# Feed-forward groups of 4, 5, 5, 5 and 3 chunks in a two-layer hybrid encoder: one more chunk multiplied by quads, another home for the down products' inputs

## Chip, cores and metric

The kernel runs on one core of a Trainium2 chip. The metric is device microseconds of one execution; "time" below is the median of three executions.

## What is computed

Two layers of an encoder trunk on 512 tokens of width 1024, all in float32. Cut to what matters:

```python
for l in range(2):
    h = rms_norm(x, attn_norm_g[l])
    proj = h @ w_in[l]                      # latents, GQA q/k/v, pool channels, gates
    merged = sum(gate_b * (branch_b @ w_branch_b[l]) for b in (mla, gqa, pool))
    x = x + merged @ w_out[l]
    hf = rms_norm(x, ffn_norm_g[l])
    u = depthwise_conv3(hf @ ffn_w_up[l]) + bias      # width 2 * 2816
    x = x + (silu(u[:, :2816]) * u[:, 2816:]) @ ffn_w_down[l]
```

The change touches the last three lines, the feed-forward part, in both layers.

## The kernel before

**Products.** Features stand on the 128 partitions, tokens along the free dimension (512). Each float32 operand is split into a high part of type float32r and a low part (the rest), and each product is three matmuls: high by high, high by low, low by high (`mm3`). So one product of 128x128 weights with 512 tokens is three matmuls of 512 columns. `HH` and `HL` hold the normed input's two parts, `wh`/`wl` and `fh`/`fl` the weights' parts. All matmuls are recorded at L526.

**Order.** The program is written out by hand, engine by engine, while a model of the engines' clocks (`Clock`) runs beside it: a side chain (`chain`, started `after` some microseconds) puts its instructions on DVE, ACT and POOL when that model's time has come. It sets only the order; on the chip the engines wait for each other by semaphores.

**Feed-forward, in 22 chunks of 128 columns of the gate half and 128 of the value half.** The chunks are cut into groups by `SIZES`, five of them. Those of the first group are "plain": two units of 8 products of 512 tokens each, 48 matmuls of 512 columns a chunk. All later chunks are "formed": the width of 1024 is paired off into four quads (two feature blocks by two halves of the tokens), and each quad takes seven products of 256 tokens in place of eight, by sums and differences of weights and of inputs. That is 7 x 4 x 3 = 84 matmuls of 256 columns a chunk. The sums of the inputs (`tf`, `hn`, `tt`) are made once a layer by `build_forms`, a quad at a time, as soon as the quad's two feature blocks are there; those of the weights by `w_form`, chunk by chunk. For three of the seven forms the low part is made by POOL issuing a transfer that adds the raw weights to minus the high part (`fl<-raw`, L438; the same for `wl<-raw` of other weights).

**Down products.** Each chunk's activations (`act`, or `ah` and `al`: high and low) meet 8 blocks of `ffn_w_down`. A group's down products, 8 per chunk, are dealt out among the next group's forms, behind the forms 22, 2, 4 and 3; those of the last group and 2 of the 8 output blocks of the group before it (`KEEP`) stand at the end of the layer. `keep_act` gives each chunk's activations a place: `PLACE[g] + i` below `ROOM` is one of 12 pieces of the four tiles of pool `mp` (which hold q and k in the attention), two per chunk; others go to `ah` from pool `wp` (tiles of 528 floats) and `al` from the slots `sp` (512 floats).

**Weights.** `_stream` sets the order in which the raw weights come over SP's queue. A formed chunk's four blocks are slots of their own; during the plain chunks the first of these are pulled ahead, one per plain unit. The split of weights runs 6 units ahead of TensorE in the feed-forward part (`LAF`).

**The norm.** The output projection's eight blocks m (`ps_acc`, `ps_ST`, `ps_AV` in turn) end in `resid` (`XM`), then `HH`, `HL` and the squares (`sqt`, summed into `sq` on POOL). `norm_begin` transposes the sum (`sqT`) and reduces it to `prt`; `norm_finish` puts a small matmul of `prt` between those of a plain unit when the model's time is `D_SUM` past `prt` (`D_FIRST` for the first norm of all), and from it come the per-token factors (`fac`, `rbc`), which scale the plain and formed results after the matmuls. So TensorE goes on with unscaled inputs while the norm is worked out. The norms are numbered `gen` 0 to 3: 0 and 2 ahead of the attention, 1 and 3 ahead of the feed-forward part.

Of the kernel before, what the change touches and what calls it, by code (L numbers as in the profile page):

```python
# [11 lines left out]
F32R = mybir.dt.float32r  # L12
# [6 lines left out]
P = 128  # L19
T = 512  # L20
# [10 lines left out]
WIDE = 528  # L31
# [10 lines left out]
PRE_A = 16  # L42
PRE_B = 8
LA, LAP, LAF = 3, 4, 6
SIZES = (5, 5, 5, 4, 3)
PLACE = (0, 5, 0, 5, 0)
ROOM = 6
KEEP = 2
FORMS = ("11", "12", "1", "22", "2", "4", "3")
# [8 lines left out]
D_SUM, D_FIRST = 2.0, 2.4  # L58
# [52 lines left out]
def _groups():  # L111
    e = np.cumsum(SIZES)
    return [(int(b - n), int(b)) for n, b in zip(SIZES, e)]


def _ffn():
# [4 lines left out]
    for g, (c0, c1) in enumerate(_groups()):  # L121
        dealt = len(late) - (KEEP * SIZES[g - 1] if g == len(SIZES) - 1 else 0)
        for n, c in enumerate(range(c0, c1)):
# [14 lines left out]
def _layer_units():  # L138

    r = _widths()  # L140
    for tok in _ffn():
        if tok[0] == "u":
            r += [("u", T), ("p", T), ("next",)]
        elif tok[0] == "f":
            r.append(tok)
        elif (tok[2] * SIZES[tok[1]] + tok[3]) % 4 == 0:
            r.append(("u" if tok[1] < len(SIZES) - 1 else "p", T))
    return r


def _stream():
# [4 lines left out]
    for kind, *u in _layer_units() * L:  # L156
        if kind == "next":
            plain = (plain + 1) % (2 * SIZES[0])
            if plain and plain >= 2 * SIZES[0] - 8:
# [49 lines left out]
class Clock:  # L209
# [37 lines left out]
    def done(self, *key):  # L247
        self.ready[key] = self.fin + self.SEM

    def need(self, *keys):  # L250
        for k in keys:
            while k not in self.ready:
                self.pop()
            self.to(self.ready[k])
# [4 lines left out]
    def chain(self, *steps, after=0.2):  # L259

        def go(n, source=None):
            if n == len(steps):
                return
            keys, fn = steps[n] if isinstance(steps[n], tuple) else ((), steps[n])
            late = [self.ready.get(k, self.now + 0.5) for k in keys]
            if late and max(late) > self.now:
                self.at(max(late) - self.now, lambda: go(n))
                return
            self.fin, self.source, self.last = self.now, source, None
            fn()  # L270
            source, self.source = self.last, None
            self.at(max(0.0, self.fin - self.now), lambda: go(n + 1, source))
        self.at(after, lambda: go(0))
# [65 lines left out]
def trunk(ctx: ExitStack, tc: tile.TileContext, x, w, prm, gb, cst, out):  # L339
    nc = tc.nc  # L340
    ctx.enter_context(tc.manual_schedule())
    ck = Clock()
    at, need, done, chain = ck.at, ck.need, ck.done, ck.chain
# [3 lines left out]
    cp = ctx.enter_context(tc.tile_pool(name="cp", bufs=1))  # L347
    rawp = ctx.enter_context(tc.tile_pool(name="rawp", bufs=RAW))
    hlp = ctx.enter_context(tc.tile_pool(name="hlp", bufs=LA + 3))
    sp = ctx.enter_context(tc.tile_pool(name="sp", bufs=NSLOT))  # L350
    wp = ctx.enter_context(tc.tile_pool(name="wp", bufs=NWIDE))
    sm = ctx.enter_context(tc.tile_pool(name="sm", bufs=2))
# [3 lines left out]
    uid = [0]  # L356

    def slot(name, dt=F32):
        uid[0] += 1
        t = sp.tile([P, SLOT], dt, tag="s", name=f"{name}_{uid[0]}")  # L360
        return t
# [5 lines left out]
    def small(name, shape, dt=F32, bufs=2):  # L367
        uid[0] += 1
        t = sm.tile(shape, dt, tag=name, name=f"{name}_{uid[0]}", bufs=bufs)
        return t  # L370
# [4 lines left out]
    def ps(tag):  # L375
        while not banks[tag]:
            ck.pop()
        ck.to(heapq.heappop(banks[tag]))
        uid[0] += 1
        t = pp.tile([P, T], F32, tag=tag, name=f"ps_{tag}_{uid[0]}", bufs=nbank[tag])  # L380
        return t
# [8 lines left out]
    def free(tag):  # L390
        heapq.heappush(banks[tag], ck.fin + ck.SEM)

    def f(ap):
        return ap.bitcast(F32)
# [130 lines left out]
    def mm(o, lhsT, rhs, start, stop, again=False):  # L525
        PE.matmul(o, lhsT=lhsT, rhs=rhs, start=start, stop=stop, skip_group_check=again)  # L526
        n = rhs.shape[-1]
        ck.to(ck.now + (n / 2400.0 + 0.0133 if st["ffn"] else max(0.107, n / 2370.0)))
# [20 lines left out]
    keep = cp.tile([P, 1], F32, tag="keep", name="keep")  # L549


    mp = ctx.enter_context(tc.tile_pool(name="mp", bufs=4))

    prms = []
    for l in range(L):
        t = cp.tile([P, NPRM], F32, tag=f"prm{l}", name=f"prm{l}")
# [60 lines left out]

    def norm_finish(gen, out, force=False):

        if gen not in parts or not (force or ck.ready.get(("prt", gen), 1e9) + (D_SUM if gen else D_FIRST) <= ck.now):  # L620
            return
        need(("prt", gen))
        s2 = ps("S")
        mm(s2[:, :16], C[:, C_GRP:C_GRP + P], parts.pop(gen), True, True)
        a, a4 = small("fac", [P, 16]), small("fac4", [P, 16])
        rt, rbc = out["rt"], out["rbc"] = small("rt", [P, 4]), slot("rbc")

        def mean():
            V.tensor_scalar(a, s2[:, :16], 1.0 / D, EPS, ALU.mult, ALU.add)
            free("S")  # L630

        def tokens():
            V.tensor_tensor(a4, a, C[:, C_SEL:C_SEL + 16], ALU.mult)
            V.tensor_reduce(rt, a4.rearrange("p (b g) -> p b g", g=4), AX.X, ALU.add)
            done("rt", gen)

        def rows():
            V.transpose(rbc[:, :T].rearrange("p (j r) -> p j r", r=32), bc(a.unsqueeze(2), [P, 16, 32]))
            done("rbc", gen)

        chain(mean, lambda: G.tensor_tensor(a, a, bc(mhalf, [P, 16]), ALU.pow), tokens, rows, after=0.3)
# [13 lines left out]
    parts = {}  # L655

    def bc(ap, shape):
        return ap.to_broadcast(shape)
# [26 lines left out]
    def layer(l, sq, xsrc):  # L685
# [3 lines left out]
        def col(i):  # L689
            return pr[:, i:i + 1]  # L690
# [146 lines left out]
        for g in range(4):  # L837
            acc = ps(ptags[g])
            for n, _ in enumerate(feat_major(acc, G1)):
                norm_finish(G1, nrm, g == 1 and n == 7)  # L840
            chain(*pool_steps(g, acc, ptags[g]))
# [748 lines left out]
        def build_forms(q):  # L1590
            a, b = slot("hn")[:, :T], slot("hn")[:, :T]
            lo, hi = slice(0, 256), slice(256, 512)
            t = (slot("tt")[:, :T], slot("tt")[:, :T])

            def whole():
                for k, z in ((2 * q, a), (2 * q + 1, b)):
                    V.tensor_scalar(z, XM[:, k, :], col(PRM_FG + k), None, ALU.mult)

            def sums():
                V.tensor_tensor(t[0][:, lo], a[:, hi], a[:, lo], ALU.subtract)  # L1600
                V.tensor_tensor(t[1][:, lo], b[:, hi], a[:, hi], ALU.subtract)
                V.tensor_tensor(t[0][:, hi], b[:, hi], t[0][:, lo], ALU.subtract)
                V.tensor_tensor(t[1][:, hi], b[:, lo], t[0][:, hi], ALU.subtract)

            def halves_of(name):
                i, h = {"1": (0, lo), "2": (0, hi), "3": (1, lo), "22": (1, hi)}[name]
                d = slot("tf", F32R)[:, :T]
                forms[name, q] = d[:, lo], d[:, hi]

                def low():  # L1610
                    V.tensor_tensor(d[:, hi], t[i][:, h], f(d[:, lo]), ALU.subtract)
                    done("tf", l, name, q)
                return [lambda: A.activation(d[:, lo], t[i][:, h], AF.Copy), low]

            for name, k, h in (("11", 2 * q, lo), ("12", 2 * q + 1, lo), ("4", 2 * q + 1, hi)):
                forms[name, q] = HH[:, k, h], HL[:, k, h]
                done("tf", l, name, q)
            chain(whole, sums, *[z for name in ("1", "2", "22", "3") for z in halves_of(name)], after=2.0)

        for m in range(KC):  # L1620
            tag = tags[m % 3]
            acc = ps(tag)
            for kc in range(KC):
                if kc % 4 == 0:
                    wh, wl = wnext()
                need(("mrg", l, kc))
                ws = slice((kc % 4) * P, (kc % 4) * P + P)
                mm3(acc, wh[:, ws], wl[:, ws], merged[kc][0][:, :T], merged[kc][1][:, :T], kc == 0, kc == KC - 1)

            def resid(m=m, acc=acc, tag=tag):  # L1630
                V.scalar_tensor_tensor(XM[:, m, :], acc, 0.5, XM[:, m, :], ALU.mult, ALU.add)
                free(tag)

            chain(resid, *norm_steps(G2, m, col(PRM_FG + m), sq),
                  *[lambda m=m: build_forms(m // 2)] * (m % 2))
# [14 lines left out]
        def keep_act(c):  # L1650
            g = next(i for i, (c0, c1) in enumerate(groups) if c0 <= c < c1)
            i = c - groups[g][0]
            n = 2 * (PLACE[g] + i)
            if n < 2 * ROOM:
                return places[n], places[n + 1]
            uid[0] += 1
            return wp.tile([P, WIDE], F32R, tag="w", name=f"ah_{uid[0]}")[:, :T], slot("al", F32R)[:, :T]

        def convolve(c, part, u):
            ci = c + part * FC  # L1660
# [353 lines left out]
```

## Time and profile before

| | |
|---|---|
| time, median of 3 executions | 1552.65 us (1552.56 to 1552.98) |
| the profiled execution | 1550.6 us |
| its span, first to last instruction | 1548.8 us, 1.8 us shorter |
| granted TensorE clock, mean | 1.000 |
| matmuls in the trace | 8265 |
| feed-forward part of layer 0 | from about 426.4 to 776.3 us of the span |
| of layer 1 | from about 1196.5 us to the end |

In the profile's rows, PE is a matmul on TensorE, PEld a weight load that runs beside it, DVE, ACT and POOL are the other engines, and SP issues transfers. A timeline row has the start in us, the time taken, engine, line, operation, output and inputs, the shape and the number merged into the row; in brackets stands the idle time ahead of it and what ended that. The ends of matmuls are modelled, so what a matmul costs in a stream is read from start to start. A windows row has, for a stretch, each engine's busy time and number of instructions, the granted clock, the share of the DMA engines that was busy, and GB/s.

### The profile page before, as it was taken

The numbers are of one execution on the slowest core, as the hardware profiler recorded it, in microseconds if no ns is written. First come the engines' busy times: TensorE is split into PE (matmuls) and PEld (weight loads), VectorE is DVE, ScalarE is ACT, GpSimd is POOL, SyncE is SP. The second block draws the span as 40 slices with busy tenths as digits, with TensorE's granted clock in tenths as the row PEclk, the third lists the DMA queues.
The fourth block names the chain that finished last, engine by engine and source line by source line (L and its number), as shares of the span: only waits on it lengthen the run. The fifth ranks groups of instructions, "written<-read, shape, count | busy, mean of one in ns | idle before, by whom it ended". The sixth has DMA issues, their size and how long they took to land.

```text
span 1548.8 us, 24353 instructions
## 1 busy us (share of the span) xinstructions
PE 1542.1 (100%) x8265; PEld 1341.3 (87%) x8265; DVE 1156.3 (75%) x1936; ACT 1066.5 (69%) x1994; POOL 775.3 (50%) x828
## 2 busy tenths in 40 slices
PE   9999999999999999999999999999999999999999
PEld 8888888888878999999898888888888899999997
DVE  6877886776687887877756678868667778888785
ACT  5557875877657877777644577758776677777772
POOL 3984886753453323222488648776535432222223
PEclk9999999999999999999999999999999999999999
DMA  5432344658968878886434323447598688787853
GB/s 203 123 120 82 88 123 141 162 128 207 225 164 195 197 169 181 197 192 143 128 128 131 111 75 92 125 144 175 117 216 213 169 205 186 180 187 177 212 116 102
DMA packets 138509, 241.26 MB, mean 156 GB/s; under 512 B 30864, under 2 KB 53392, under 8 KB 138384
## 3 DMA queue, kind: packets, MB, share of 16 engines
q1 hardware_dynamic: 91152, 162.93, 34.0%
q0 software_dynamic: 42336, 76.56, 28.8%
q8 instruction: 65, 1.06, 0.3%
q10 hardware_dynamic: 4896, 0.21, 0.2%
q14 instruction: 60, 0.49, 0.1%
HBM read 149.41 MB, written 13.63 MB: 105 GB/s over the span
## 4 chain that ended last, share of the span: by engine, by line
PE 92%; DVE 3%; DMA 2%; ACT 1%; issue 1%; POOL 1%; SPq 0%; ACTq 0%; POOLq 0%; DVEq 0%
PE ps_acc L526 40%; PE ps_AV L526 17%; PE ps_ST L526 15%; PE ps_S L526 10%; PE ps_mi L526 9%; DMA raw<-w 1%; DVE tf L307 1%; ACT wh L300 0%; SPq L862 0%; POOL wl L307 0%; DVE ctl L311 0%; DVE win L307 0%; ACT mx L300 0%; DVE wl L307 0%; POOL fac L307 0%
## 5 line engine op out<-in xcount | busy, mean ns | idle before, releaser
L438 POOL DMA_DIRECT2D wl<-raw x192 | 172.4, 903 | 383.1 <-ACT sx L300 163.7
L307 POOL TENSOR_TENSOR wl<-raw,wh 128x512 fp32r<-128x512 f32 (+2 forms) x171 | 219.9, 1294 | 179.4 <-ACT wh L300 171.7
L300 ACT ACTIVATE wh<-raw 128x512 fp32r<-128x512 f32 (+2 forms) x453 | 266.3, 605 | 55.6 <-DMA raw<-w 13.2
L438 POOL DMA_DIRECT2D fl<-raw x102 | 89.0, 873 | 155.2 <-ACT fl L300 62.6
L526 PE MATMUL ps_acc<-HH,wh 128*128 128x512 f32 x416 | 163.2, 392 | 0.5 <-DVE XM L311 0.4
L526 PE MATMUL ps_acc<-HL,wh 128*128 128x512 f32 x416 | 162.8, 391 | 0.3 <-DVE HL L311 0.3
L526 PE MATMUL ps_acc<-HH,wl 128*128 128x512 f32 x416 | 162.7, 391 | 0.0
L311 DVE SCALAR_TENSOR_TENSOR a<-u,prm,a 128x511 f32<-128x511 f32 x176 | 133.5, 761 | 33.5 <-ACT a L300 32.5
L300 ACT ACTIVATE wl<-wh 128x512 fp32r<-128x512 f32 x192 | 120.6, 628 | 6.1
L315 DVE TENSOR_REDUCE nm<-ps_S 128x1 fp32r<-128x512 f32 x128 | 87.8, 686 | 44.6 <-PE ps_S L526 43.7
L300 ACT ACTIVATE a<-u,prm 128x512 f32<-128x512 f32 x88 | 71.2, 811 | 57.2 <-DVE u L307 57.1
L526 PE MATMUL ps_acc<-tf,wh 128*128 128x256 f32 x544 | 100.1, 282 | 0.0
L526 PEld LDWEIGHTS ps_acc<-tf,wh 128*128 128x128 f32 x544 | 88.5, 189 | 6.2
L526 PEld LDWEIGHTS ps_acc<-HH,wh 128*128 128x128 f32 x416 | 78.4, 188 | 16.6 <-issue 0.7
L526 PEld LDWEIGHTS ps_acc<-HH,wl 128*128 128x128 f32 x416 | 78.2, 188 | 16.8
L526 PEld LDWEIGHTS ps_acc<-HL,wh 128*128 128x128 f32 x416 | 78.3, 188 | 16.6 <-DVE HL L311 0.6
L307 DVE TENSOR_TENSOR wl<-raw,wh 128x512 fp32r<-128x512 f32 (+2 forms) x91 | 66.2, 729 | 22.9 <-ACT wh L300 22.7
L526 PE MATMUL ps_AV<-HH,wh 128*128 128x256 f32 (+1 forms) x248 | 82.2, 331 | 0.0
L526 PE MATMUL ps_AV<-HH,wl 128*128 128x256 f32 (+1 forms) x248 | 82.1, 331 | 0.0
L526 PE MATMUL ps_AV<-HL,wh 128*128 128x256 f32 (+1 forms) x248 | 82.1, 331 | 0.0
L526 PE MATMUL ps_acc<-tf,wl 128*128 128x256 f32 x272 | 76.7, 282 | 0.0
L307 DVE TENSOR_TENSOR pl<-ps_ST,ph 128x512 fp32r<-128x512 f32 x86 | 58.3, 682 | 15.6 <-ACT ph L300 11.4
(426 smaller groups left out, 4975.3 us busy)
## 6 DMA issues: line engine op xcount, KB each, us to landing
raw<-w SPq DMA_DIRECT2D x160, 512.0 KB, 3.9
wl<-raw POOLq DMA_DIRECT2D x188, 256.0 KB, 4.4
raw<-w SPq DMA_DIRECT2D x140, 256.0 KB, 4.4
fl<-raw POOLq DMA_DIRECT2D x102, 256.0 KB, 5.6
raw<-w SPq DMA_DIRECT2D x14, 384.0 KB, 3.0
XM<-x SPq DMA_DIRECT2D x16, 256.0 KB, 4.5
dtq<-tr SPq DMA_DIRECT2D x16, 192.0 KB, 2.0
dtk<-tr SPq DMA_DIRECT2D x16, 192.0 KB, 3.3
```

Source lines behind the costliest of these rows:

```text
L300: return self.eng.activation(out, in_, func, **k)
L307: return self.eng.tensor_tensor(out, *a)
L311: return self.eng.scalar_tensor_tensor(out, *a)
L315: return self.eng.tensor_reduce(out, in_, *a, **k)
L438: nc.gpsimd.dma_start(f(lo), r, accum_op=ALU.add)
L526: PE.matmul(o, lhsT=lhsT, rhs=rhs, start=start, stop=stop, skip_group_check=again)
```

## The change

`SIZES` goes from 5, 5, 5, 4, 3 to 4, 5, 5, 5, 3: in each layer one chunk of the first group is no longer plain but formed, and the fourth group has five chunks. `PLACE` follows: the second group's first chunk now has place 4, so that two of its five chunks fit below `ROOM`. The pool `mp` is opened ahead of the slots and no longer behind them, and activations without a place take two slots, none of the wide tiles. The distance of the feed-forward norms' small matmul goes from 2.0 to 2.4 us of the model's time, and the sums of the third and fourth quad's inputs are started 8 us behind their block's chain in place of 2.

```diff
-SIZES = (5, 5, 5, 4, 3)
-PLACE = (0, 5, 0, 5, 0)
+SIZES = (4, 5, 5, 5, 3)
+PLACE = (0, 4, 0, 5, 0)
...
     hlp = ctx.enter_context(tc.tile_pool(name="hlp", bufs=LA + 3))
+    mp = ctx.enter_context(tc.tile_pool(name="mp", bufs=4))
     sp = ctx.enter_context(tc.tile_pool(name="sp", bufs=NSLOT))
     wp = ctx.enter_context(tc.tile_pool(name="wp", bufs=NWIDE))
...
-    mp = ctx.enter_context(tc.tile_pool(name="mp", bufs=4))
-
...
-        if gen not in parts or not (force or ck.ready.get(("prt", gen), 1e9) + (D_SUM if gen else D_FIRST) <= ck.now):
+        if gen not in parts or not (force or ck.ready.get(("prt", gen), 1e9) + (D_FIRST if gen in (0, 1, 3) else D_SUM) <= ck.now):
...
-            chain(whole, sums, *[...], after=2.0)
+            chain(whole, sums, *[...], after=2.0 if q < 2 else 8.0)
...
-            uid[0] += 1
-            return wp.tile([P, WIDE], F32R, tag="w", name=f"ah_{uid[0]}")[:, :T], slot("al", F32R)[:, :T]
+            return slot("ah", F32R)[:, :T], slot("al", F32R)[:, :T]
```

Nothing outside the two feed-forward parts and the norms ahead of them changes its order on any engine but for a few transfers of SP at the parts' ends. In the built programs 8261 matmuls become 8333: in each layer 48 of 512 columns go and 84 of 256 come. Per layer the down products between the forms go from 144 to 142, at the end from 32 to 34. The four `mp` tiles move from byte 204640 of each partition to byte 93824. The first leaves 32 when divided by 64, the second 0, and all twelve places have the same rest, since they lie 2048 bytes apart. `HH`, `HL` and all slots have rest 0, before and now; the wide tiles, 2112 bytes apart, rest 0 by 64 but 0 or 64 by 128.

**DVE at the end of layer 0's output projection.** `XM<-ps_acc` and `XM<-ps_ST` are here blocks m = 6 and 7; `hn`, `tt` and `tf` the third quad's sums. Before:

```order
L311 SCALAR_TENSOR_TENSOR XM<-ps_acc_4604,XM 128x512
L311 SCALAR_TENSOR_TENSOR HL<-XM,prm_91,HH 128x512
L319 TENSOR_SCALAR hn_4671<-XM,prm_91 128x512
L319 TENSOR_SCALAR hn_4672<-XM,prm_91 128x512
L307 TENSOR_TENSOR tt_4673<-hn_4671 128x256
L307 TENSOR_TENSOR tt_4674<-hn_4672,hn_4671 128x256
L307 TENSOR_TENSOR tt_4673<-hn_4672,tt_4673 128x256
L307 TENSOR_TENSOR tt_4674<-hn_4672,tt_4673 128x256
L311 SCALAR_TENSOR_TENSOR XM<-ps_ST_4660,XM 128x512
L307 TENSOR_TENSOR tf_4675<-tt_4673,tf_4675 128x256
L311 SCALAR_TENSOR_TENSOR HL<-XM,prm_91,HH 128x512
```

Now:

```order
L311 SCALAR_TENSOR_TENSOR XM<-ps_acc_4606,XM 128x512
L311 SCALAR_TENSOR_TENSOR HL<-XM,prm_91,HH 128x512
L311 SCALAR_TENSOR_TENSOR XM<-ps_ST_4662,XM 128x512
L311 SCALAR_TENSOR_TENSOR HL<-XM,prm_91,HH 128x512
L319 TENSOR_SCALAR hn_4673<-XM,prm_91 128x512
L319 TENSOR_SCALAR hn_4674<-XM,prm_91 128x512
L307 TENSOR_TENSOR tt_4675<-hn_4673 128x256
L307 TENSOR_TENSOR tt_4676<-hn_4674,hn_4673 128x256
L307 TENSOR_TENSOR tt_4675<-hn_4674,tt_4675 128x256
L307 TENSOR_TENSOR tt_4676<-hn_4674,tt_4675 128x256
L331 STREAM_TRANSPOSE sqT_4714<-sq_4307 128x512
L315 TENSOR_REDUCE prt_4715<-sqT_4714 128x16
```

The last block's residual and low part stand ahead of the six instructions of the third quad's sums; its `tf`, four instructions of which two stood ahead of `sqT`, stand behind `prt`. Layer 1 has the same order. On PE the matmul of `prt` stands 45 matmuls behind the output projection's last one, where it stood 39 behind.

**POOL at the second to third formed chunk of layer 0.** All rows are transfers: `fl` a formed chunk's low parts, `wl` those of a row of four down blocks. Before:

```order
L438 DMA fl_5296<-raw_4802 128x512
L438 DMA fl_5316<-raw_4867 128x512
L438 DMA fl_5354<-raw_4964 128x512
L438 DMA wl_5372<-raw_5106 128x512
L438 DMA wl_5445<-raw_5106 128x512
L438 DMA fl_5491<-raw_5209 128x512
L438 DMA fl_5511<-raw_5220 128x512
```

Now:

```order
L439 DMA fl_5209<-raw_4708 128x512
L439 DMA fl_5228<-raw_4795 128x512
L439 DMA fl_5263<-raw_4970 128x512
L439 DMA wl_5309<-raw_5017 128x512
L439 DMA fl_5370<-raw_5119 128x512
L439 DMA fl_5397<-raw_5130 128x512
```

The first formed group, with 32 down products in place of 40 behind its 35 products, has one `wl` less between two chunks here.

More of the change, by code (lines that the diff above doesn't have):

```diff
@@ L1617, in build_forms @@
                 done("tf", l, name, q)
-            chain(whole, sums, *[z for name in ("1", "2", "22", "3") for z in halves_of(name)], after=2.0)
+            chain(whole, sums, *[z for name in ("1", "2", "22", "3") for z in halves_of(name)], after=2.0 if q < 2 else 8.0)
         for m in range(KC):
```

## The prediction

> **What bounds the kernel now.** I read the page's busy shares first, then its chain of work that ended last, then stretches of the feed-forward part, then single rows of the timeline.
>
> ```profile
> PE 1542.1 (100%) x8265; PEld 1341.3 (87%) x8265; DVE 1156.3 (75%) x1936; ACT 1066.5 (69%) x1994; POOL 775.3 (50%) x828
> ...
> PE 92%; DVE 3%; DMA 2%; ACT 1%; issue 1%; POOL 1%; SPq 0%; ACTq 0%; POOLq 0%; DVEq 0%
> ```
>
> TensorE is busy all the time and makes 92% of the chain. The stretches of layer 0's plain chunks (from 439), its first formed group (from 483) and a later formed one (from 644) say the same, with the busy time of PE, PEld, DVE, ACT and POOL, then granted clock, DMA share and GB/s:
>
> ```profile
> 439.00:483.00 44.00, 44.00 (x197) 36.45 (x196) 30.60 (x44) 29.38 (x48) 21.05 (x18) 1.00 0.74 181
> 483.00:564.00 81.00, 80.99 (x564) 75.31 (x563) 67.56 (x114) 61.85 (x116) 21.66 (x25) 1.00 0.84 187
> ```
>
> PE misses 0.01 us in 81 at a granted clock of 1.00. So the time is the sum of the spacings from one matmul's start to the next, plus the few waits; a matmul less is a spacing less, as long as the other engines and the transfers keep up. DVE is closest behind (67.56 of 81), with the DMA engines busy 0.84 of that stretch.
>
> All terms below are changes to the profiled execution, 1550.6 us with a span of 1548.8; it lies 2.05 below the median of 1552.65, and I carry the same difference to the median.
>
> **A. One chunk a layer formed in place of plain.** Matmul starts at the plain chunks' second to fifth, and at a formed chunk with its down products behind it:
>
> ```profile
> 439.01 0.39 PE L526 MATMUL ps_AV<-HH,wh 128*128 128x512 f32 x1
> ...
> 482.56 0.28 PE L526 MATMUL ps_acc<-HH,fh 128*128 128x256 f32 x1
> ...
> 529.76 0.28 PE L526 MATMUL ps_acc<-HH,fh 128*128 128x256 f32 x1
> ...
> 535.51 0.63 PE L526 MATMUL ps_mi<-act,wh 128*128 128x512 f32 x2
> 536.90 0.40 PE L526 MATMUL ps_acc<-tf,wh 128*128 128x256 f32 x2
> ...
> 545.36 0.28 PE L526 MATMUL ps_acc<-HH,fh 128*128 128x256 f32 x1
> ```
>
> From 439.01 to 482.56 lie four plain chunks, 192 matmuls: 43.55 / 192 = 226.8 ns each, 10.89 us a chunk. From 529.76 to 535.51 lie 48 matmuls of 256 columns: 119.8 ns each, so 84 make 10.06. The chunk to 545.36 took 15.60 in all, which leaves 5.54 for its 24 down matmuls, 231 ns each. The plain chunk costs 10.89, the formed one 10.06: 0.83 a layer, **1.7 us** less in all. The down products are equally many before and after.
>
> The Trainium skill, in "TensorE: Matmul & The Clock Gate" under "Back-to-back issue gap", gives an isolated spacing of N / 2.4 + 2.5 ns. By that the two widths would take 215.8 and 109.2 ns and term A would be 2.4 us, an estimate from that page; the rows lie some 11 ns above it at either width, so the rows decide.
>
> What covers the added work: the added chunk's sums on DVE, splits on ACT and transfers run beside TensorE. In the 81 us row, 5.19 chunks of 15.6 long, they take 13.0 us of DVE, 11.9 of ACT and 13.1 of DMA time a chunk. The first formed group now spreads 32 down products over five chunks, 6.4 each: 10.06 + 6.4 x 3 x 0.231 = 14.5 us a chunk, which still covers 13.0, though with DVE at 90%.
>
> **B. The down inputs' byte offset.** Rows of the end's act products (72 matmuls, left rest 32 by 64), the output projection (192, rest 0), and a run of nine of each kind behind narrower matmuls:
>
> ```profile
> 759.53 0.62 PE L526 MATMUL ps_acc<-act,wh 128*128 128x512 f32 x2
> ...
> 776.32 0.34 PE L526 MATMUL ps_acc<-wh,HH 128*128 128x384 f32 x1
> ```
>
> ```profile
> 382.83 0.39 PE L526 MATMUL ps_acc<-mgh,wh 128*128 128x512 f32 x1
> ...
> 426.35 0.39 PE L526 MATMUL ps_acc<-HH,wh 128*128 128x512 f32 x1
> ```
>
> ```profile
> 170.73 0.40 PE L526 MATMUL ps_acc<-HH,wh 128*128 128x512 f32 x1
> ...
> 172.80 0.39 PE L526 MATMUL ps_ST<-qa,ka 128*128 128x512 f32 x1
> ...
> 647.66 0.63 PE L526 MATMUL ps_mi<-act,wh 128*128 128x512 f32 x2
> ...
> 649.76 0.28 PE L526 MATMUL ps_AV<-HH,wh 128*128 128x256 f32 x1
> ```
>
> The act stream takes 16.79 / 72 = 233.2 ns a matmul, the other 43.52 / 192 = 226.7: 6.5 ns dearer. With the kept blocks some 102 matmuls a layer stand in such long runs: 0.66 a layer, 1.3 in both. In short runs the price is less plain: nine of HH take 2.07, nine of act 2.10, 30 ns a run or about 3 a matmul; the six at 535.51 took 1.39, while six at 226.7 with a seam of 30 ns (the nine of HH hold 2.07 - 9 x 0.2267 = 0.03) would take the same, so I take 10 ns for a six. A layer has 6 nines and 58 sixes between forms now: 0.18 + 0.58 = 0.76, or 1.5 in both. Together **2.8 us**. Nothing has shown that it is the byte offset that does it and not the order of operands; the ends are 0 and 6.5 ns on all 1056 down matmuls, 6.9 us. I take the middle, nearest to the long runs' and nines' own rows.
>
> The page "SBUF — State Buffer" of the Trainium skill, under "Door 1: The DMA port swizzle (why `[64,N]` ≈ `[32,N]`)", speaks against this term: on-chip memory has lines of 16 bytes, and rests of 32 and 0 both begin one, so by it a move to another rest changes nothing. No run here shows a line's size; its outcome is the first rival.
>
> **C. The norm ahead of the feed-forward part.** PE in layer 0's first plain chunk and DVE from the output projection's end on:
>
> ```profile
> 430.88 0.39 PE L526 MATMUL ps_acc<-HH,wl 128*128 128x512 f32 x1
> ...
> 432.19 0.50 PE L526 MATMUL ps_acc<-HL,wh 128*128 128x512 f32 x1 [0.28 <-DVE HL L311]
> 432.53 0.40 PE L526 MATMUL ps_acc<-HH,wl 128*128 128x512 f32 x1
> ...
> 435.95 0.39 PE L526 MATMUL ps_ST<-HH,wl 128*128 128x512 f32 x1
> ...
> 436.61 0.40 PE L526 MATMUL ps_S<-prt,C 128*128 128x16 f32 x2 [0.27 <-DVE prt L315]
> ```
>
> ```profile
> 425.46 0.88 DVE L319 TENSOR_SCALAR hn<-XM,prm 128x512 f32<-128x512 f32 x2
> 426.26 1.52 DVE L307 TENSOR_TENSOR tt<-hn 128x256 f32<-128x256 f32 x1
> ...
> 429.92 0.68 DVE L311 SCALAR_TENSOR_TENSOR XM<-ps_ST,XM 128x512 f32<-128x512 f32 x1
> ...
> 431.39 0.75 DVE L311 SCALAR_TENSOR_TENSOR HL<-XM,prm,HH 128x512 fp32r<-128x512 f32 x1 [0.46 <-ACT HH L300]
> ...
> 434.95 0.70 DVE L331 STREAM_TRANSPOSE sqT<-sq 128x512 f32<-128x512 f32 x1
> ...
> 435.89 0.67 DVE L315 TENSOR_REDUCE prt<-sqT 128x16 f32<-128x512 f32 x1
> ```
>
> Three spacings from 430.88 to 432.53 take 1.65 us, not 3 x 0.227 = 0.68: 0.97 of waiting for block 7's HH and HL, whose residual stood behind the third quad's six sums on DVE from 425.46 to 429.92. The output projection's last product began before 426.35, so with the sums moved behind it the residual can run from about 426.6 and HL, 1.47 us behind it and 0.75 long, is there by 428.9; TensorE asks for it after 431. The wait goes. The second one, 435.95 to 436.61, is 0.66 for a 0.23 spacing: 0.43. Now the six sums (4.5 us, 425.46 to 429.92) follow HL from 428.9 on, then `sqT` and `prt` (0.70 and 0.67) with no `tf` between: prt is there near 434.8. It was asked for at 436.18 (435.95 and one spacing); with 0.97 less ahead of it and six matmuls more that becomes 436.6. In layer 1:
>
> ```profile
> 1205.13 0.39 PE L526 MATMUL ps_ST<-HH,wl 128*128 128x512 f32 x1
> ...
> 1205.57 0.40 PE L526 MATMUL ps_S<-prt,C 128*128 128x16 f32 x2
> ```
>
> 0.44 for 0.23, 0.21 to win. Sum **1.6 us**; the ends are 0, if as much waits elsewhere, and 1.6. Late next would be the third quad's own sums, but only formed chunks use them, from 471.7 on (482.56 - 10.89).
>
> **D. New waits for low halves.** POOL's transfer issue and its use by PE, at the second formed chunk and in the steady state:
>
> ```profile
> 494.11 0.86 POOL L438 DMA_DIRECT2D fl<-raw  x1 [1.11 <-ACT sx L300]
> ...
> 552.99 0.86 POOL L438 DMA_DIRECT2D fl<-raw  x1 [0.58 <-ACT sx L300]
> ```
>
> ```profile
> 499.84 0.28 PE L526 MATMUL ps_ST<-HL,fh 128*128 128x256 f32 x1
> 500.13 0.39 PE L526 MATMUL ps_ST<-HH,fl 128*128 128x256 f32 x1
> ...
> 562.63 0.28 PE L526 MATMUL ps_ST<-HH,fl 128*128 128x256 f32 x1
> ```
>
> ```profile
> DMA to landing us min/median/max: 3.3/5.6/9.2
> ```
>
> At 500.13 TensorE waited 0.29 - 0.12 = 0.17 for a transfer issued 6.02 before. By the program's order its issue and its use stand 46 half-width and 18 full matmuls apart (46 x 0.1198 + 18 x 0.231 = 9.67 us), and 44 and 15 after the change (8.74): the down products that stood between are gone. That is 0.93 less, so a wait of about 1.1 in layer 0 and 0.9 in layer 1. At the fourth formed chunk the distance goes from 47 and 18 (9.79) to 38 and 10 (6.86). The steady state leaves 9.64 from issue to use, 4.0 over the median landing; 2.9 of that goes, and the median still fits. If this one lands at the longest, 9.2, it costs 2.3. So the ends are 0 and (1.1 + 2.3) x 2 = 6.9; I take **+2.0**, the second chunk in both layers, nearest to the wait seen. Behind a late `fl` stands all that is queued on TensorE. One more edge is near: in the trace the last plain chunk's low half came
>
> ```profile
> 492.55 0.69 DVE L307 TENSOR_TENSOR act<-a,act 128x512 fp32r<-128x512 f32 x1 [1.20 <-ACT act L300]
> ```
>
> at 493.24, 10.7 us behind the plain chunks' end, and in the new order the fourth chunk's first down product stands about as far behind it; a wait there is in the 2.0.
>
> Sum: -1.7 - 2.8 - 1.6 + 2.0 = -4.1. Profiled 1546.5, median **1548.5 us**.
>
> **Rivals.** *Offsets do nothing.* The dearer act stream comes of the operand's kind or the weights' arrival, not of its place; for it, the sixes above show little, and so do three of `ah` and `al`, at rest 0 by 64:
>
> ```profile
> 567.40 0.39 PE L526 MATMUL ps_mi<-ah,wh 128*128 128x512 f32 x1
> ...
> 568.10 0.28 PE L526 MATMUL ps_acc<-tf,wh 128*128 128x256 f32 x1
> ```
>
> 0.70 / 3 = 233 ns, as act's; against it, 3 x 226.7 with the seam is 0.71 too, and the 72 in a row have no seam. Without B: -1.3, 1551.3 us. *Slower: the formed chunk has a floor.* If DVE, ACT or the DMA engines, and not TensorE, set a formed chunk's length F, then the first group's five chunks in each layer can't go below it: 10 x (F - 14.5) is lost. The waits of D would lie within that floor, so the base is 1546.5 at the median; it turns slower by over 0.2% (1555.75) from F = 15.4 on, and at the 15.6 measured above it costs 11: 1557.5. For it: DVE 90% and DMA 0.90 in 14.5 us chunks. Against it: PE's 80.99 of 81, which leaves no sign of such a floor. *Late low halves cost about 5*, with two of the fourth chunk's transfers slow: 1551.5. *The offset pays on all 1056 matmuls*: 6.9 in place of 2.8, 1544.4.
>
> **How the numbers follow.** Forecast 0.47; offsets do nothing 0.20; low halves 0.17; full offset gain 0.10; floor 0.06. The range is 1544.5 to 1553.0: it takes in the first two rivals and, nearly, the full gain, and leaves out the floor and the ends of D on top of a missing B. What a measurement of this kernel can tell from no change is about 0.2%, 3.1 us, so faster is below 1549.55: the forecast's larger part and the full gain, with a share of the rest, 0.60; same 0.34, mostly the two middle rivals; slower 0.06, the floor.
>
> **What would show it.** A: the added chunk's 84 spacings at 119.8 ns, the first group's chunks near 14.5 us, PE still at 100% there. B: the layer's last 72 act matmuls in 16.3 us in place of 16.79. C: no idle for HL or prt on PE ahead of 437 or in layer 1. D: the wait rows of `fl` near 1 us at the second formed chunk and none at the fourth. The forecast is wrong if the act stream stays at 233 ns, if `fl` waits pass 3 us in all, or if DVE ends the idle time of PE in the first formed group.

## The result and the profile after

The changed kernel took 1547.12 us (median of 7 executions, 1546.13 to 1549.66); the kernel before, timed beside it, 1552.56 (7 executions, 1551.36 to 1552.98). The ratio is 0.9969, with a 95% interval of 0.9958 to 0.9981. That is 5.4 us between the medians; the forecast was 4.1.

The two profiled executions are a bad pair for this: the one before took 1550.6 and lies under all seven of its timings, the one after took 1548.79, the second longest of its seven. They differ by 1.8 us. Further profiles below show which of their waits come in every execution and which only in some.

The page after: busy shares, and the chain that ended last.

```profile
PE 1537.7 (99%) x8337; PEld 1342.7 (87%) x8337; DVE 1169.6 (76%) x1960; ACT 1073.5 (69%) x2010; POOL 768.6 (50%) x826
...
PE 88%; issue 4%; DMA 3%; DVE 2%; POOL 2%; ACT 1%; SPq 0%; ACTq 0%; POOLq 0%; DVEq 0%
```

TensorE is still the engine that sets the time. Its first formed group, as a stretch (busy PE, PEld, DVE, ACT, POOL, then clock, DMA share, GB/s) and as the starts of its first four chunks:

```profile
471.00:528.00 57.00, 57.00 (x410) 53.84 (x409) 48.87 (x84) 45.46 (x86) 15.60 (x18) 1.00 0.81 183
```

```profile
470.66 0.28 PE L527 MATMUL ps_acc<-HH,fh 128*128 128x256 f32 x1
...
484.88 0.28 PE L527 MATMUL ps_acc<-HH,fh 128*128 128x256 f32 x1
...
499.09 0.28 PE L527 MATMUL ps_acc<-HH,fh 128*128 128x256 f32 x1
...
514.00 0.28 PE L527 MATMUL ps_acc<-HH,fh 128*128 128x256 f32 x1
```

PE misses nothing in 57 us; three chunks take 43.34, or 14.45 each, with DVE at 86% (48.87 of 57).

The last 72 act matmuls of layer 0 now take 774.20 - 757.88 = 16.32 us, 226.7 ns each; before they took 16.79:

```profile
757.88 0.62 PE L527 MATMUL ps_acc<-act,wh 128*128 128x512 f32 x2
...
774.20 0.33 PE L527 MATMUL ps_acc<-wh,HH 128*128 128x384 f32 x1
```

At the norm ahead of the feed-forward part, DVE works off block 7 before the third quad's sums, and PE's small matmul of prt waits for nothing (0.36 us from 436.42 to 436.78, where the same two steps took 0.9 before):

```profile
426.64 0.69 DVE L311 SCALAR_TENSOR_TENSOR XM<-ps_ST,XM 128x512 f32<-128x512 f32 x1 [0.21 <-PE ps_ST L527]
428.52 1.36 DVE L311 SCALAR_TENSOR_TENSOR HL<-XM,prm,HH 128x512 fp32r<-128x512 f32 x1 [1.19 <-ACT HH L300]
429.81 3.68 DVE L319 TENSOR_SCALAR hn<-XM,prm 128x512 f32<-128x512 f32 x2
```

```profile
436.42 0.39 PE L527 MATMUL ps_ST<-HH,wl 128*128 128x512 f32 x1
436.65 0.29 PE L527 MATMUL ps_S<-prt,C 128*128 128x16 f32 x2
436.78 0.48 PE L527 MATMUL ps_ST<-HH,wh 128*128 128x512 f32 x1
```

This execution has three waits that the first profile of before has not. In layer 0 a `wl` of a late plain chunk (459.58 to 460.09, 0.28 over a spacing). In layer 1 the fifth formed chunk's second `fl`, which POOL issued at 1291.05 and which took 8.12 us to land:

```profile
1297.29 0.28 PE L527 MATMUL ps_ST<-HL,fh 128*128 128x256 f32 x1
1299.21 0.39 PE L527 MATMUL ps_ST<-HH,fl 128*128 128x256 f32 x1 [1.64 <-DMA fl<-raw]
```

1.92 us where 0.12 is a spacing. And at the end of each layer, where the last kept block (m = 7) takes the bank `ps_S`; here are PE, DVE and POOL in layer 0:

```profile
753.17 0.39 PE L527 MATMUL ps_mi<-ah,wl 128*128 128x512 f32 x1
754.31 0.74 PE L527 MATMUL ps_S<-act,wh 128*128 128x512 f32 x2 [0.75 <-DVE XM L307]
```

```profile
749.38 2.88 DVE L311 SCALAR_TENSOR_TENSOR a<-u,prm,a 128x511 f32<-128x511 f32 x2 [2.85 <-ACT a L300]
...
753.57 0.68 DVE L307 TENSOR_TENSOR XM<-ps_S,XM 128x512 f32<-128x512 f32 x1
```

```profile
748.72 2.99 POOL L307 TENSOR_TENSOR wl<-raw,wh 128x512 fp32r<-128x512 f32 x2 [1.04 <-ACT wh L300]
```

`ps_S` still holds block 5, whose last matmul started at 749.77. Its residual stands on DVE behind two convolution steps that took 2.88 us beside POOL's two `wl` (such a pair took 1.54 at 754.53, with POOL idle), so TensorE waits 1.14 - 0.23 = 0.91. The same 1.14 stands in layer 1 at 1522.60.

### The profile page after: what moved, and what is told of

Same layout as the page of the kernel before. It is cut to its first block, busy times and chain, and to the rows that moved or that the text cites. A ratio compares the mean times of both kernels' runs of the same rounds, so it can differ in the third digit from the quotient of the medians.

```text
span 1547.0 us, 24549 instructions
## 1 busy us (share of the span) xinstructions
PE 1537.7 (99%) x8337; PEld 1342.7 (87%) x8337; DVE 1169.6 (76%) x1960; ACT 1073.5 (69%) x2010; POOL 768.6 (50%) x826
## 4 chain that ended last, share of the span: by engine, by line
PE 88%; issue 4%; DMA 3%; DVE 2%; POOL 2%; ACT 1%; SPq 0%; ACTq 0%; POOLq 0%; DVEq 0%
PE ps_acc L527 40%; PE ps_AV L527 16%; PE ps_ST L527 15%; PE ps_S L527 9%; PE ps_mi L527 8%; DMA raw<-w 1%; POOL wl L307 1%; DMA fl<-raw 1%; POOL win L307 0%; DMA wl<-raw 0%; DVE a L311 0%; ACT wh L300 0%; DMA qb<-nm 0%; DVE ctl L311 0%; DVE u L307 0%
## 5 line engine op out<-in xcount | busy, mean ns | idle before, releaser
L307 POOL TENSOR_TENSOR wl<-raw,wh 128x512 fp32r<-128x512 f32 (+3 forms) x167 | 213.5, 1287 | 169.0 <-ACT wh L300 150.8
L439 POOL DMA_DIRECT2D fl<-raw x108 | 94.4, 874 | 168.6 <-ACT fl L300 62.7
L527 PE MATMUL ps_acc<-HH,wh 128*128 128x512 f32 x400 | 156.8, 392 | 0.4 <-DVE XM L311 0.4
L527 PE MATMUL ps_acc<-HH,wl 128*128 128x512 f32 x400 | 156.6, 391 | 0.1
L527 PE MATMUL ps_acc<-HL,wh 128*128 128x512 f32 x400 | 156.5, 391 | 0.0
L300 ACT ACTIVATE wl<-wh 128x512 fp32r<-128x512 f32 (+1 forms) x188 | 118.1, 628 | 5.9
L527 PE MATMUL ps_acc<-tf,wh 128*128 128x256 f32 x576 | 106.2, 282 | 0.0
L527 PEld LDWEIGHTS ps_acc<-tf,wh 128*128 128x128 f32 x576 | 94.3, 191 | 6.0
L527 PE MATMUL ps_acc<-tf,wl 128*128 128x256 f32 x288 | 81.5, 283 | 0.0
L300 ACT ACTIVATE fl<-fh 128x512 fp32r<-128x512 f32 x108 | 68.4, 633 | 3.4
```

The source lines that it names most:

```text
L300: return self.eng.activation(out, in_, func, **k)
L307: return self.eng.tensor_tensor(out, *a)
L439: nc.gpsimd.dma_start(f(lo), r, accum_op=ALU.add)
```

## The experiments

Each kernel was timed beside the kernel before on the same chip, 5 to 12 executions of it; of the last one below there is a single execution. Ratios are to the kernel before.

**The offset alone.** 32 bytes ahead of the last pool of the kernel before, nothing else:

```diff
+    pad = ctx.enter_context(tc.tile_pool(name="pad", bufs=1)).tile([P, 8], F32, tag="pad", name="pad")
     mp = ctx.enter_context(tc.tile_pool(name="mp", bufs=4))
```

> The kernel before with 32 bytes put ahead of pool mp: its tiles move from byte 204640 to 204672 of each partition, rest 0 by 64 and by 128, and nothing else changes (ah and al stay where they were). Theory (the byte offset sets the spacing): the layer's last 72 act matmuls take 16.3 us in place of 16.79, nines 2.07 in place of 2.10, the whole 1.5 to 2.3 us less. Rival (kind or order of the operands, or the region of memory): the 72 stay at 16.8 and the time within 0.5 us.

Measured: 1550.78 against 1552.14, ratio 0.9992 (0.9983 to 1.0000). The 72 act matmuls:

```profile
759.06 0.39 PE L526 MATMUL ps_acc<-act,wh 128*128 128x512 f32 x1
...
775.38 0.33 PE L526 MATMUL ps_acc<-wh,HH 128*128 128x384 f32 x1
```

16.32 us, the changed kernel's value, with the tiles still in their old region and every operand and order as before. Over all 1064 down matmuls of both layers the spacings sum to 243.67 us, 1.9 less than the 245.57 of before. So it is the offset that sets the spacing. In time it is 1.4 us, a little under the 1.5 to 2.3 expected, and the interval reaches no change: this execution also waits 0.84 us (499.04 to 500.00 for a spacing of 0.12), and 0.70 in layer 1, for `fl` at the second formed chunk, where the first profile of before waits 0.17.

**The norm edits alone,** in the kernel before:

```diff
-(D_SUM if gen else D_FIRST)
+(D_FIRST if gen in (0, 1, 3) else D_SUM)
...
-after=2.0)
+after=2.0 if q < 2 else 8.0)
```

> The kernel before with the two norm edits alone (2.4 us for the feed-forward norms' small matmul, the third and fourth quad's sums 8 us later). Theory: the waits for HL of block 7 and for prt go in layer 0 and the one for prt in layer 1, 1.2 to 1.9 us less, the lower end if the plain chunks of layer 0 then wait 0.4 for a wl as they did in the changed kernel. Rival: the sums moved behind run into the norm's chain and the wait only moves: within 0.3 us.

Measured: 1549.53 against 1552.14, ratio 0.9980 (0.9972 to 0.9989), 2.6 us less: more than the 1.2 to 1.9 expected. In its trace TensorE has no wait of over 0.1 us in either feed-forward part; the row of prt reads as in the changed kernel:

```profile
438.20 0.29 PE L526 MATMUL ps_S<-prt,C 128*128 128x16 f32 x2
438.34 0.48 PE L526 MATMUL ps_ST<-HH,wh 128*128 128x512 f32 x1
```

**The groups alone,** in the kernel before:

```diff
-SIZES = (5, 5, 5, 4, 3)
-PLACE = (0, 5, 0, 5, 0)
+SIZES = (4, 5, 5, 5, 3)
+PLACE = (0, 4, 0, 5, 0)
```

> The kernel before with SIZES and PLACE alone (activations without a place still in ah of the wide tiles). Theory: 1.4 us less for the formed chunks, but 0.9 a layer of waiting for XM of ps_S at the layer's end, and 0 to 2 a layer for fl at the fifth formed chunk: +0.4 in sum, between -0.2 and +3. Rival (the fl wait and the end wait belong to the norm edits or to the places): -1.4.

Measured: 1553.71 against 1552.14, ratio 1.0009 (1.0001 to 1.0017), within what was expected. One more formed chunk a layer, by itself, makes the kernel no faster. Its waits in layer 0 and, below, in layer 1 (total us, times, longest):

```profile
PE ps_acc L526 <- ACT HH L300: 0.7, 1, 0.7
PE ps_S L526 <- DVE XM L307: 0.7, 1, 0.7
PE ps_ST L526 <- DMA wl<-raw: 0.6, 1, 0.6
PE ps_ST L526 <- DMA fl<-raw: 0.5, 1, 0.5
...
PE ps_S L526 <- DVE XM L307: 0.6, 1, 0.6
PE ps_ST L526 <- ACT wh L300: 0.6, 1, 0.6
PE ps_ST L526 <- DMA fl<-raw: 0.5, 1, 0.5
```

The end wait for XM is there without the norm edits and the new offsets, so it comes with the groups. New are the `fl` and `wh` waits at the first two formed chunks; from start to start, `fl` costs 0.68 us at the second one in layer 0 and 0.65 in layer 1. The norm, which waits in layer 0 (`HH` above), does not wait for `HH` or `HL` in layer 1, just as it did not in the profile that the prediction read.

**The kernel before once more,** with no edit.

> The kernel before, unchanged, for a second profile. Theory: the same time within 0.1%; if its profiled execution is nearer to the median of 1552.6 than the first one (1550.6), the 2 us between them show as waits of TensorE for fl or wl transfers whose landing varies from execution to execution. Rival: the spacing of the matmuls itself varies (sum over all matmuls 0.1% longer, no wait).

Measured: 1552.58, ratio 0.9999 (0.9990 to 1.0008), its profiled execution 1552.96. Neither expectation held: of the 2.4 us between the two profiles only 0.3 is a late transfer, and none is spacing. The largest part, 1.2, is the norm in layer 1, which waits here as it does in layer 0 (the rest is 0.4 at layer 0's norm and 0.7 ahead of layer 0's feed-forward part, less 0.2 elsewhere):

```profile
1201.88 0.39 PE L526 MATMUL ps_acc<-HH,wl 128*128 128x512 f32 x1
1202.39 0.50 PE L526 MATMUL ps_acc<-HH,wh 128*128 128x512 f32 x1
1203.18 0.50 PE L526 MATMUL ps_acc<-HL,wh 128*128 128x512 f32 x1 [0.28 <-DVE HL L311]
1203.52 0.40 PE L526 MATMUL ps_acc<-HH,wl 128*128 128x512 f32 x1
```

1.64 us for three spacings of 0.23. In the profile that the prediction read, layer 1 had no such wait. The cause stands in DVE's third-quad sums and in POOL beside them; first this execution:

```profile
1196.44 0.87 DVE L319 TENSOR_SCALAR hn<-XM,prm 128x512 f32<-128x512 f32 x2
1197.23 1.52 DVE L307 TENSOR_TENSOR tt<-hn 128x256 f32<-128x256 f32 x1
1198.68 1.51 DVE L307 TENSOR_TENSOR tt<-hn,hn 128x256 f32<-128x256 f32 x1
...
1196.87 1.60 POOL L307 TENSOR_TENSOR wl<-raw,wh 128x512 fp32r<-128x512 f32 x1 [1.94 <-ACT wh L300]
1198.44 1.46 POOL L307 TENSOR_TENSOR sq<-sq,sqt 128x512 f32<-128x512 f32 x1
```

and the one that the prediction read:

```profile
1195.63 0.88 DVE L319 TENSOR_SCALAR hn<-XM,prm 128x512 f32<-128x512 f32 x2
1196.42 0.42 DVE L307 TENSOR_TENSOR tt<-hn 128x256 f32<-128x256 f32 x1
1196.76 0.42 DVE L307 TENSOR_TENSOR tt<-hn,hn 128x256 f32<-128x256 f32 x1
...
1196.06 2.60 POOL L307 TENSOR_TENSOR wl<-raw,wh 128x512 fp32r<-128x512 f32 x1 [1.95 <-ACT wh L300]
```

The same two sums take 1.52 and 1.51 us beside POOL's adds, or 0.42 each, and then it is POOL's that is long (2.60 in place of 1.60). POOL's `wl` starts 0.43 us behind DVE's `hn` in both, so what decides is finer than the rows show. The Trainium skill, "SBUF — State Buffer", "Who interferes with whom", says that a DVE instruction with two inputs in on-chip memory contends with a GpSimd (POOL) instruction that reads it, and that the order of issue decides who is blocked. On the contention these rows agree; on the order they don't settle it, since POOL's `wl` starts 0.36 us ahead of DVE's first sum in both executions and is the long one in only one of them.

**The changed kernel without its norm edits:**

```diff
-(D_FIRST if gen in (0, 1, 3) else D_SUM)
+(D_SUM if gen else D_FIRST)
...
-after=2.0 if q < 2 else 8.0)
+after=2.0)
```

> The changed kernel with its two norm edits undone. Theory (the norm edits take away HL's and prt's waits in both layers, 1.7 to 1.8 us each in a usual execution): 1550.5 us, 3.4 more than the changed kernel, with the three waits back in the first plain chunk of both layers. Rival (the norm is worth the 1.6 of the prediction and the rest of the 5.4 us comes of the groups and the offsets): 1548.7.

Measured: 1553.75 against 1551.60, ratio 1.0011 (1.0002 to 1.0020). By the ratios that is 0.42%, 6.5 us, above the changed kernel: both expectations too low. In its profile the norm's three waits are back in both layers, and with them waits at the first two formed chunks; layer 0:

```profile
476.31 0.28 PE L527 MATMUL ps_AV<-tf,wl 128*128 128x256 f32 x1
477.19 0.48 PE L527 MATMUL ps_ST<-tf,fh 128*128 128x256 f32 x2 [0.61 <-ACT wh L300]
...
489.14 0.28 PE L527 MATMUL ps_ST<-HL,fh 128*128 128x256 f32 x1
489.80 0.39 PE L527 MATMUL ps_ST<-HH,fl 128*128 128x256 f32 x1 [0.39 <-DMA fl<-raw]
```

0.88 and 0.66 where 0.12 is a spacing. A likely reading, not taken apart, is that with one plain chunk less, what DVE, ACT and POOL are behind with from the norm meets the first formed chunks. The feed-forward parts of the two layers take 702.1 us here, 695.1 in the changed kernel's second profile. This kernel is the groups alone plus the new places, and in the two profiles the down matmuls' spacings sum to 243.4 here and 245.7 there, end waits left out. Yet its time is no shorter (1.0011 against 1.0009), nor are its feed-forward parts (702.1 against 702.4): waits take the 2.3 us back, layer 1's norm alone 1.2.

**Which half of the norm edits.** The changed kernel with the first of those two pieces alone undone, so that the distance is 2.0 again,

> The changed kernel with the small matmul's distance of the feed-forward norms back at 2.0, the later quads' sums still 8 us behind. Theory (the sums' place on DVE takes the waits away, the distance little): the waits for HL stay away, one for prt of 0.2 to 0.5 a layer comes back at most: +0.4 to +1.0 against the changed kernel. Rival (the distance does it): over 2.5 more than the changed kernel.

and with the second alone undone, so that the sums start 2 us behind their block again:

> The changed kernel with the third and fourth quad's sums started 2 us behind their block again, the distance at 2.4. Theory: the waits for HL of block 7 come back in both layers (1.0 to 1.4 each) and with them those at the first formed chunks (about 1.6 a layer): 4 to 6 more than the changed kernel, 1551 to 1553. Rival (the waits at the first formed chunks belong to the distance): 2 to 2.8 more.

Measured on one chip, where the changed kernel took 1547.51: with the distance back 1549.62 (ratio to before 0.9977, 0.9967 to 0.9987), 2.1 more; with the sums back 1555.27 (1.0015, 1.0006 to 1.0024), 7.8 more. So the sums' place on DVE carries it, and more than expected. But in the profile with the sums back the wait for HL is there in layer 0 alone, not in both layers; most of the rest is `wl` late at plain chunks (1.5 and 1.4 us in the two layers) and waits at formed chunks (1.6 and 2.0). The distance is worth more than the 0.4 to 1.0 expected, too, though three of its eight executions lie among the changed kernel's five: besides 0.3 for prt in layer 1, a `wl` of the plain chunks is late in both layers (0.78 and 0.77). Layer 0 with the distance back:

```profile
459.66 0.39 PE L527 MATMUL ps_acc<-HL,wh 128*128 128x512 f32 x1
460.67 0.50 PE L527 MATMUL ps_acc<-HH,wl 128*128 128x512 f32 x1 [0.62 <-DMA wl<-raw]
```

1.01 us where 0.23 is a spacing; with the sums back the same place takes 1.35 (460.57 to 461.92). The profile with the distance back holds 1.2 of `fl` waiting at the fifth formed chunk as well, which is no part of the edit (below). Why this `wl` follows the norm's place was not taken apart further.

**Another bank for the last kept block.** In the changed kernel:

```diff
-state["tag"] = tags[m % 3] if ends else ("mi", "S")[m % 2]
+state["tag"] = tags[m % 3] if ends else "ST" if g == len(groups) - 2 and m == KC - 1 else ("mi", "S")[m % 2]
```

> The changed kernel with the last kept block (m = 7 of the fourth group) accumulated in ps_ST in place of ps_S. Theory (at the layer's end TensorE waits 0.9 us a layer for XM of ps_S, which stands on DVE behind two a's that ran beside POOL): the wait goes in both layers, 1.8 us less, 1545.3. Rival (the act products behind it wait for the same DVE chain): the wait moves to the last group's first act, within 0.4 us of the changed kernel.

Measured: 1544.75 against 1551.60, ratio 0.9960 (0.9947 to 0.9972). The end waits are gone in both layers; left are 0.34 and 0.24 for `fl` at the fifth formed chunk. In time the bank alone is not clear of noise: the changed kernel has ratios of 0.9969 and 0.9964, whose intervals overlap this one's.

**And another deal,** with that bank:

```diff
+now = late[:(6, 7, 6, 7, 6)[n] if g == 1 else dealt * (n + 1) // (c1 - c0) - dealt * n // (c1 - c0)]
```

> The same, and the first formed group's 32 down products dealt 6, 7, 6, 7, 6 over its chunks in place of 6, 6, 7, 6, 7, which takes the shortest distance from an fl transfer's place to its use from 6.86 to 7.6 us. Theory (the fifth formed chunk's fl is late in some executions, 0 to 1.8 us a layer): 0 to 1.5 us less than with ps_ST alone, and no wait over 0.3 for fl. Rival (another chunk is late in its place): the same time, with an fl wait at the third or fourth formed chunk.

> The kernel with ps_ST for the last kept block and the deal 6, 7, 6, 7, 6, once more, beside the changed kernel on one chip. Theory: 1.8 to 3.5 us below the changed kernel, no wait of TensorE between the plain chunks and the layer's end but 0.15 for the small matmul. Rival (the 3 us between the two lie in the chips): within 1 us of it.

Measured: 1544.05 against 1551.60, ratio 0.9956 (0.9943 to 0.9968), and again 1544.65 against 1552.77, 0.9948 (0.9936 to 0.9961), 2.9 us below the changed kernel on that chip. The feed-forward parts of both layers as stretches of the second of these:

```profile
426.00:772.30 346.30, 346.30 (x2236) 316.52 (x2235) 283.34 (x465) 253.32 (x466) 116.50 (x120) 1.00 0.76 176
1192.50:1538.70 346.20, 346.20 (x2243) 316.84 (x2242) 277.30 (x460) 244.34 (x450) 107.82 (x114) 1.00 0.75 173
```

PE is busy in all of them: nothing is left there but matmul spacings. The residual of `ps_S` still comes late on DVE, but the next block no longer needs its bank:

```profile
752.54 0.61 PE L527 MATMUL ps_ST<-act,wh 128*128 128x512 f32 x2
...
752.71 0.68 DVE L307 TENSOR_TENSOR XM<-ps_S,XM 128x512 f32<-128x512 f32 x1
```

What the deal adds to the bank alone, 0.7 us, is less than the intervals' width; the profiles without any `fl` wait speak for it.

**The changed kernel once more,** with no edit.

> The changed kernel once more, beside the next on one chip: 1547.1 within 0.1%. Theory (the fl wait at the fifth formed chunk varies by execution and the 0.9 for XM of ps_S doesn't): its profile shows 0.9 in both layers and another fl wait than 1.8 in layer 1. Rival: the 1.8 is there again.

Measured: 1547.51 against 1552.77, ratio 0.9964 (0.9951 to 0.9978); its profiled execution took 1547.08. The 0.91 for XM is there in both layers (752.63 to 753.77 and 1520.85 to 1521.99 for a spacing of 0.23), the `fl` wait of 1.8 is gone (0.10 left). The wait for XM stands in both layers of all six profiles of these groups that keep the bank, 0.81 to 0.91 us each.

**Another rest.** 96 bytes of padding in the kernel before. Its one execution, 1554.77 us, says nothing of the time; what is read is the spacing.

```diff
+    pad = ctx.enter_context(tc.tile_pool(name="pad", bufs=1)).tile([P, 24], F32, tag="pad", name="pad")
     mp = ctx.enter_context(tc.tile_pool(name="mp", bufs=4))
```

> The kernel before with 96 bytes ahead of pool mp: rest 0 by 64 but 64 by 128. If 64 bytes are the unit, the 72 act matmuls at the layer's end take 16.3 us as with 32 bytes of padding; if 128 are, they stay near 16.8. The rule of 16-byte lines would give one and the same for all three places.

```profile
761.92 0.39 PE L526 MATMUL ps_acc<-act,wh 128*128 128x512 f32 x1
...
778.40 0.34 PE L526 MATMUL ps_acc<-wh,HH 128*128 128x384 f32 x1
```

16.48 us, 228.9 ns each: neither of the two expected values. Between the forms the six of act take 1.406 us on average, against 1.388 at rest 0 by 128 and 1.397 at the rest of before (32 by 64, which is 96 by 128). So a multiple of 64 is not enough, and 128 was, in both places tried.

## Why the prediction was right, point by point

The sum came out near, but two of its terms were wrong and one was missing, and the missing one nearly cancelled D's error. Compared here are two executions close to their medians, the second profile of before (1552.96) and the second of after (1547.08). Their feed-forward parts take 700.4 and 695.1 us, 5.3 apart:

| term, both layers | predicted | measured | from |
|---|---|---|---|
| A, one chunk formed | -1.7 | -1.44 | sum of spacings: 96 of 512 columns less, 21.89; 168 of 256 more, 20.44 |
| B, offset | -2.8 | -2.34 | sum of spacings of the 1064 down matmuls, 245.56 to 243.22 |
| C, norm waits | -1.6 | -3.4 | waits ahead of the second plain chunk, 3.68 to 0.31 |
| D, late `fl` and `wl` | +2.0 | -0.1 | other waits, 0.69 to 0.54 |
| end of the layer | none | +2.0 | 1.02 a layer, for XM of `ps_S` |

**A** held in size and in reason. The added chunk's half-width matmuls took 121.7 ns each (20.44 / 168) where the prediction had 119.8. The rival of a floor under a formed chunk falls: the chunks with 18 down matmuls took 14.21 us (484.88 to 499.09) at PE busy in full.

**B** held: the 72 act matmuls fell to 226.7 ns as forecast, nines and sixes by 29 and 9 ns where 30 and 10 stood (the traces of before have 8 nines and 59 sixes a layer, the prediction 6 and 58, which is 0.1 us in both layers). The padding alone showed 1.9 of it; the remaining 0.4 fits `ah`, which left the wide tiles, half of them at rest 64 by 128. No kernel moved it alone, but the sixes of `ah` and `al` stay at 1.394 us in the padded kernel, where those of act fall to 1.388; with the new places they take 1.387 (the changed kernel without its norm edits) against 1.395 (the groups alone). The rival "offsets do nothing" is refuted by the padded kernel, in which only the rest changed. By the 16-byte lines of the Trainium skill's page "SBUF — State Buffer" ("Door 1: The DMA port swizzle (why `[64,N]` ≈ `[32,N]`)") all rests tried here would be alike, since each begins a line; the measured 226.7, 228.9 and 233.2 ns are not, and the measurement decides.

**C** had the right mechanism and about half its size. The step that failed is "in layer 1 ... 0.21 to win": it took one execution's row for the kernel's. In that execution DVE's sums went ahead of POOL's add; in the second profile POOL's went ahead and layer 1 waits 1.6 us, nearly as long as layer 0 (2.0). Seven profiles have the sums at their old place. Layer 0 waits for `HH` or `HL` in all of them, layer 1 in four (the second of before, both paddings, the changed kernel without its norm edits). In the other three (the first of before, the groups alone, the sums back) DVE's two sums take 0.42 us each and POOL's add 2.60. So this wait comes and goes, and one profile can't price it. That the first profile lay 2 us below its median was a sign, and the prediction carried it along as a constant; but it is no sure one, since the profile of the groups alone lies at its median and lacks the wait, too. In time the two norm edits are worth 2.6 alone (3.1 by the ratio), and some 6.5 with the groups changed: then they take away the waits at the first formed chunks also. The prediction treated C and D as independent terms to be added; they are not. The reserve was small as well: prt came at 436.29, not near 434.8, since DVE's two `hn` took 3.68 us beside POOL in place of 0.88, and it was 0.36 us ahead of its use.

**D** failed in both its steps. At the second formed chunk of the changed kernel no wait came: there the prediction put the program's distance (9.67, then 8.74) in place of the time. The transfer before was issued 3.65 us later than its place in the program (6.02 to its use); after, POOL was less late and it had 6.74, with 1.74 to spare:

```profile
479.81 0.86 POOL L439 DMA_DIRECT2D fl<-raw  x1 [1.11 <-ACT sx L300]
```

```profile
486.55 0.28 PE L527 MATMUL ps_ST<-HH,fl 128*128 128x256 f32 x1
```

Where the norm edits are missing the wait did come, at about half the forecast size: 0.68 and 0.65 us with the groups alone, 0.55 and 0.45 in the changed kernel without its norm edits (there, in layer 0, issued 5.32 ahead of its use and landing after 5.82). So the step overlooked that C's edits let POOL catch up. At the other chunk, the distance of 6.86 is that of the fifth formed chunk, not of the fourth (9.1), against 10.4 before; so 3.5 us went there, not 2.9. That is where `fl` is late, by 0 to 1.8 us as the landing varies. The upper rival ("two slow transfers, about +5") happened by a third, in one execution.

**What the sum did not have** is the end wait, +2.0. The prediction counted the kept blocks' products and not their bank: m = 7 reuses `ps_S`, and DVE's residual of block 5 stands behind two convolution steps that are slow beside POOL (2.88 us, 1.54 without). The prediction put this wait at nothing without a reason. The wait is the size that D was given, so that the total came out well by luck: -4.1 forecast, -5.3 in the feed-forward parts of these two profiles (-5.9 in their whole times), -5.4 in the medians.

## What to carry to other kernels

Before an edit is priced from one profile, compare that execution with the timings: a profile that lies below all of them, here 2 us below their median, may lack a wait that other executions have, and one place to look for it is where DVE and POOL read memory at the same moment. A second profile of the same kernel shows it. Where TensorE is busy all the time, count matmul spacings for what an edit takes away, and then go along every bank and buffer that the new order reuses, since the waits that come back stand there; at this kernel's end that was a bank, and another tag took its 2.0 us of waiting away. An edit that lets DVE, ACT and POOL catch up can be worth more beside one that leans on them than alone (by the ratios 6.5 us against 3.1 here).

## What the runs showed of the hardware

In this kernel's down products a streamed float32r operand of 512 columns costs 226.7 ns a matmul where its start is a multiple of 128 bytes, 233.2 where it leaves 96 by 128, and 228.9 where it leaves 64 (in the 72 in a row at the layer's end; in sixes between narrower matmuls the order of the last two turns round, 1.397 and 1.406 us). A start at a multiple of 64 bytes was not enough. The 228.9 comes from a single execution.

DVE's sum of 128x256 floats takes 0.41 to 0.42 us with POOL idle (437.27 in the first profile of before) and 1.52 beside POOL's add of 128x512; POOL's own goes from 1.60 to 2.60 when it is the one that waits. Two executions of one program, alike to 0.01 us in the distances of the rows that go into it, came out 1.2 us apart in what TensorE then waited (1.64 and 0.48 in layer 1).
